# A hybrid attention trunk: contiguous rows per partition and another load order at the start, a finer warm-up, and a later due time for the layer border's transposes

## The chip, the cores and the metric

The kernel runs on one core of a Trainium2 chip. The metric is the device time of one execution in microseconds. The engines are TensorE (PE in the profile; its weight loads are PEld), VectorE (DVE), ScalarE (ACT), GpSimd (POOL) and SyncE (SP). DMAs are issued by an engine onto its own queue (SPq, ACTq) and carried out by 16 DMA engines.

## The reference, cut to what matters

Two layers over 256 tokens of 1024 channels; then a final RMSNorm:

```python
for layer in range(2):
    h = rms_norm(x, norm_g[layer])
    proj = einsum('btd,dc->btc', h, w_in[layer])          # w_in: 1024 x 3584
    sb_q, sb_k, sb_v, sb_g, mb_q, mb_k, mb_v, mb_g, mem_q, mem_g = split(proj)
    o_sb  = stick_breaking_attention(sb_q, sb_k, sb_v) * silu(sb_g)    # 6 heads of 64
    o_mb  = moba_attention(rotary(mb_q), rotary(mb_k), mb_v) * silu(mb_g)   # 6 heads
    mk, mv = split(einsum('bmd,dc->bmc', rms_norm(mem, mem_norm_g[layer]), w_mem_kv[layer]))
    o_mem = memory_attention(mem_q, mk, mv) * silu(mem_g)  # 4 heads, 256 memory tokens
    x = x + einsum('btc,cd->btd', concat([o_sb, o_mb, o_mem]), w_out[layer])
return rms_norm(x, final_norm_g)
```

All is in fp32. Besides the inputs the kernel is given x and mem transposed (xT, memT) and `gcols`, a 128 x 32 table of the four rows of gains: columns 0 to 7 are norm_g of layer 0, with row p, column k holding gain 128k + p; columns 16 to 31 are the memory gains.

## The kernel before, in words

**Split products.** A product of fp32 matrices is made of fp32r halves: each operand is split into a high part (a rounding cast) and a low part (the operand less its high part), and high x high, high x low and low x high are added up in PSUM. The activations are kept transposed, as `T` (a tile of 128 x 8 x 512: for each of 8 slices of 128 channels the high part in 256 columns and the low part in 256). In layer 0, `T` is x^T (tile `uT`, slices called xT0 to xT7) times the gain: `scale_hi` (L595, ScalarE, L248) makes the high part, `scale_lo` (L601, VectorE, L256) the low one. The rows' RMS factor is put in later, when a finished product leaves PSUM.

**Weights in chunks.** Every weight matrix comes in chunks of 128 partitions x 768 floats (384 KB; a few are 256 KB), in the order in which PE uses them. `dma_chunk` (L387) issues the next one on SyncE through `dma` (L332, so each issue shows as L333) into one of 5 buffers `raw`. `hi_task` (L405) casts it into the high half of one of 7 buffers `hl`, on ScalarE (L246) or VectorE (L267), as the planner finds; `lo_task` (L414) subtracts on VectorE (L252) and then calls `dma_chunk` again, since the `raw` buffer is free. The first piece, sb_qk, has 768 columns, so a chunk is one slice of 128 channels; its first two slices are cut in halves of 384 columns (chunks 0 to 3, 192 KB each), and chunk 4 is slice 2, chunk 5 slice 3, and so on.

**The layout of the channels.** `"(k p)"` in L355 and L428 lets partition p of slice k hold channel 128k + p, for w_in and x^T alike. A chunk's row in a partition is one run of memory (1.5 or 3 KB), and the next partition's run lies one row of w_in (14 KB) on. For x^T a run is one row of 1 KB.

**The start.** L436 to L446 issue the first loads in this order. On SyncE: gc (the table of gains, 16 KB), xT0, xT1, chunk 2, chunk 3, xT2, chunk 4, xT3, then xT4 and xT5 in one DMA. On ScalarE's queue: chunk 0, chunk 1. xT6 and xT7, the two halves of x and the constants follow when `dma_chunk` gets to chunks 7, 8 and 13 (L396 to L403). `main` (L980) clears `junk` on VectorE (L983) and runs 7 products of 128 x 512 in bf16 on it, whose result isn't used (the warm-up). Then come the products of sb_qk, slice by slice over six PSUM banks (L1053 to L1082): in slices 0 and 1 for three banks (one half chunk) at a time, with separate products of 256 columns; from slice 2 on with products of 512 and 256 columns.

**The order of the work.** A list planner written in the kernel (`Sched`, L82) decides in which order the instructions are issued on each engine, when the program is built: each task names what it needs, and the planner keeps a clock for each engine from estimated costs and landing times. A PE instruction of a side task is put `late` ns later than it could start by these estimates: `PE_LATE` = 100, and for the transposes at the layer border `NORM_LATE` (L32, L580). On the chip each engine runs its instructions strictly in that order and waits for semaphores.

**The layer border.** After layer 0's output projection, `norm_task` (L571) makes layer 1's `T` for two halves of tokens and two halves of channels: VectorE's normalised half-row `w` (L256, stt), four transposes on PE (L235), the high part on ScalarE and the low part on VectorE. In the meantime PE works on mk and mv of layer 1, which need only the memory tokens.

Of the kernel before, what the change touches and what calls it, by code (L numbers as in the profile page):

```python
# [7 lines left out]
F32 = mybir.dt.float32  # L8
FR = mybir.dt.float32r
BF = mybir.dt.bfloat16  # L10
AF = mybir.ActivationFunctionType
OP = mybir.AluOpType
# [5 lines left out]
KT = 8  # L18
# [10 lines left out]
KORD = (0, 1, 2, 3, 4, 5, 6, 7)  # L29
LAT_SAME, LAT_CROSS = 130.0, 240.0  # L30
PE_LATE = 100.0
NORM_LATE = 1200.0  # L32
P_H0 = -8
P_RX = 1
P_M0 = 12
P_RM = 12
P_M1 = 4
# [162 lines left out]
def hybrid_trunk(ctx: ExitStack, tc: tile.TileContext, x, mem, norm_g, w_in, w_mem_kv, w_out,  # L200
                 final_norm_g, xT, memT, gcols, consts, out):
    nc = tc.nc
# [35 lines left out]
    def act(out, in_, func=AF.Copy, **kw):  # L238
        c = 0.833 * _free(in_) + (50.0 if is_psum(in_) else 93.0)
        for a in ("scale", "bias"):  # L240
            if a in kw and not isinstance(kw[a], float):
                c += 93.0
        if "accum_out" in kw:
            c += 93.0
        if func == AF.Copy and not kw:
            nc.scalar.copy(out, in_)  # L246
        else:
            nc.scalar.activation(out, in_, func, **kw)  # L248
        S.op("act", c)
# [5 lines left out]
    def stt(out, a, s, b, op0, op1):  # L255
        nc.vector.scalar_tensor_tensor(out, a, s, b, op0=op0, op1=op1)  # L256
        S.op("dve", 1.0417 * _free(out) + (69.0 if isinstance(s, float) else 130.0))
# [12 lines left out]
    def R(*eng, **kw):  # L270
        kw["eng"] = [e if isinstance(e, tuple) else (e, 0.0) for e in eng]
        return kw

    def sb(name, shape, dt=F32):
        return cpool.tile(shape, dt, name=name)
# [2 lines left out]
    xs = sb("xs", [128, 2, D])  # L278
    cst = sb("cst", [128, 512])
    gc = sb("gc", [128, 32])  # L280
    identb = sb("identb", [128, 128], BF)
    masks = sb("masks", [128, 2, 128], BF)
    negT = sb("negT", [128, 128], FR)
# [48 lines left out]
    def dma(dst, src, name=None, q=None, now=0.0):  # L332
        (q or nc.sync).dma_start(dst, src)  # L333
        if q is None:
            S.T["sp"] = max(S.T["sp"], now) + SP_ISSUE
        t = queue(_free(dst) * 4 * dst.shape[0], dst.shape[-1] * 4, now)
        if name:
            S.ready[name] = t
# [13 lines left out]

    order = []
    for l in range(DEPTH):
        wi = w_in[l].rearrange("(k p) c -> p k c", p=128)  # L355
        wm = w_mem_kv[l].rearrange("(k p) c -> p k c", p=128)
        wo = w_out[l].rearrange("(k p) c -> p k c", p=128)
        names = ORDER[l] + ["wo0", "wo1", "wo2"]
        for n in names:
            if n in COLS:  # L360
                c, w = COLS[n]
                order.append(Piece(n, l, wi[:, :, c:c + w], w))
            elif n[:2] == "wo":
                c = 384 * int(n[2])
                w = min(384, D - c)
                order.append(Piece(n, l, wo[:, :, c:c + w], w))
            else:
                c = 256 * (n == "mv")
                order.append(Piece(n, l, wm[:, :, c:c + 256], 256))
# [17 lines left out]
    def dma_chunk(now=0.0, q=None):  # L387
        j = prog["dma"]
        if j >= len(chunks):
            return  # L390
        p, kk, c, w = chunks[j]
        n = len(kk)
        dma(raws[j % RAW][:, :n * w].rearrange("p (k c) -> p k c", c=w),
            p.src[:, kk[0]:kk[0] + n, c:c + w], ("raw", j), q, now)
        prog["dma"] += 1
        if j == X67_AT:  # L396
            load_xT(6, 8, now=now)
        for t, at in enumerate((X0_AT, X1_AT)):
            if j == at:
                dma(xs[:, t, :], x_r[:, t, :], ("x", t), now=now)  # L400
        if j == CST_AT:
            dma(cst, consts[:, 0:512], "cst", now=now)
            dma(S.res["w"].items[0][2][:, :256], consts[:, 512:768], "msk", now=now)  # L403

# [20 lines left out]

    x_r = x.rearrange("b (t p) d -> p (b t) d", p=128)
    mem_r = mem.rearrange("b (t p) d -> p (b t) d", p=128)
    xT_r = xT.rearrange("(k p) t -> p k t", p=128)  # L428
    memT_r = memT.rearrange("(k p) t -> p k t", p=128)
    out_r = out.rearrange("b (t p) d -> p (b t) d", p=128)  # L430
    def load_xT(k0, k1, q=None, now=0.0):
        dma(uT[:, k0:k1, :], xT_r[:, k0:k1, :], ("xT", k0), q, now)
        for k in range(k0 + 1, k1):
            S.ready["xT", k] = S.ready["xT", k0]

    dma(gc, gcols, "gc")  # L436
    dma_chunk(q=nc.scalar)
    load_xT(0, 1)
    dma_chunk(q=nc.scalar)
    load_xT(1, 2)  # L440
    dma_chunk()
    dma_chunk()
    load_xT(2, 3)
# [148 lines left out]
            S.mark(done + (q,))  # L592
        S.mark(done)

    def scale_hi(src, need, col, H, done):  # L595
        for k in range(KT):
            yield R("act", need=[need + (k,), "gc"])
            act(H[0][:, k, :], src[:, k, :], AF.Copy, scale=gc[:, col + k:col + k + 1])
            S.mark(done + ("hi", k))

    def scale_lo(src, need, col, H, done):  # L601
        for k in range(KT):
            yield R("dve", need=[done + ("hi", k)] + [("hi", 0)] * (k == 0))
            stt(H[1][:, k, :], src[:, k, :], gc[:, col + k:col + k + 1], H[0][:, k, :].bitcast(F32),
                OP.mult, OP.subtract)
            S.mark(done + (k,))

    def scale_task(src, need, col, H, done, prio):
        S.spawn(scale_hi(src, need, col, H, done), prio, S.cur.t)
        S.spawn(scale_lo(src, need, col, H, done), prio, S.cur.t)  # L610

    def load_memT(l):
        for q in range(4):
# [366 lines left out]
    def main():  # L980
        hT, mT = Ts
        yield R("dve")
        nc.vector.memset(junk, 0.0)  # L983
        S.op("dve", 150.0)
        _, (acc,) = yield R("pe", alloc=["bank"])
        for _ in range(7):
            mm(acc, junk[:, :128], junk, True, True)
        S.free("bank", acc)
        scale_task(uT, ("xT",), 0, hT, ("h", 0), P_H0)
        for t in range(2):  # L990
            S.spawn(row_stats(2, t, xs[:, t, :], "x", rcx, rbx), P_RX)
        S.spawn(rows_done("x", "rx"), P_RX)
# [1 line left out]
        def mem_loads():  # L994
            load_memT(0)
            dma(gb, mem_r[:, 0, :], ("mem", 0), now=S.cur.t)
            scale_task(uT, ("memT", 0), 16, mT, ("mT", 0), P_M0)
            S.spawn(rows_task(3, lambda t: gb, "mem", "rm", rcm, rbm), P_RM)

        late, given = [], set()  # L1000
# [6 lines left out]
        for l in range(DEPTH):  # L1007
# [75 lines left out]
            for i, p in enumerate(ORDER[l]):  # L1083
                if l == 0 and i == MEM_AT:
                    mem_loads()
                if l == 0 and set(ORDER[0][i:]) <= {"mk", "mv"} and not late:
                    late.append(scale_task(uT, ("memT", 1), 24, hT, ("mT", 1), P_M1))
                if p == "sb_q" and l == 1:
                    yield from T_piece(p, hT, 3, hneed, lambda c, acc: evac_T(l, "sb_q", c, acc, 0.125, rb, "rx"))
                elif p == "mk":  # L1090
                    yield from T_piece("mk", mT, 2, mneed, lambda c, acc: evac_T(l, "mk", c, acc, 1.0, rbm, "rm"))
                elif p == "mv":
                    yield from N_piece("mv", mT, mneed,
                                       lambda t, acc: evac_v(l, "mv", t, acc, rcm[:, t:t + 1], 4, "rm"))
                elif p == "sb_k":
                    yield from T_piece(p, hT, 3, hneed, lambda c, acc: evac_T(l, "sb_k", c, acc, 1.0, rb, "rx"))
                elif p in ("sb_v", "mb_v"):
                    yield from N_piece(p, hT, hneed, lambda t, acc: evac_v(l, p, t, acc, rr_(t), 6, "rx"))
                elif p == "mem_q":
                    yield from T_piece(p, hT, 2, hneed,  # L1100
                                       lambda c, acc: evac_T(l, "mem_q", c, acc, 0.125, rb, "rx"))
                elif p == "mb_q":
                    yield from N_piece(p, hT, hneed, lambda t, acc: rope_task(
                        l, "mb_q", t, acc, rr_(t, True) if l == 0 else 0.125))
                elif p == "mb_k":
                    S.spawn(rope_turn(l), 2, S.cur.t)
                    yield from N_piece(p, hT, hneed, lambda t, acc: rope_task(
                        l, "mb_k", t, acc, rr_(t) if l == 0 else 1.0))
                if {"mk", "mv"} <= set(ORDER[l][:i + 1]) and not S.res["F%d" % l].items and l not in given:
                    given.add(l)  # L1110
                    for f in range(4):
                        S.free("F%d" % l, mT[2][:, 2 * f:2 * f + 2, :].rearrange("p k c -> p (k c)").bitcast(F32))
                if p in GATES:
                    yield from T_piece(p, hT, sum(map(len, GATES[p])), hneed, lambda c, acc: gate_evac(
                        l, p[:-2], c, acc, [g for g in GATES[p] if c in g][0]))

            if l == 0 and not late:
                late.append(scale_task(uT, ("memT", 1), 24, hT, ("mT", 1), P_M1))

            def xneed(k):  # L1120
                return [("mx", l, k)]
# [71 lines left out]
```

## Time and profile before

| | |
|---|---|
| time, median of 3 runs | 279.24 us (278.77 to 279.37) |
| profiled execution | 279.69 us |
| its span, first to last instruction | 277.9 us |
| mean granted TensorE clock | 0.997 |
| PE busy | 97 % of the span |
| VectorE busy | 83 % |
| ScalarE busy | 66 % |
| DMA, mean rate | 218 GB/s |

The profile is of one execution, whose time outside the span is 1.8 us. In its rows a group reads: start, duration, engine, line, operation, output <- inputs, shape and count; the bracket behind has the engine's idle time before it and what ended that. L230 is the helper of all products, L333 that of all DMAs, L246, L248, L252, L256 and L267 those of casts, scalings and subtractions, so groups are told apart by their tiles.

### The profile page before, as it was taken

Reading aid. Unit: us, or ns where it says so; the run is one execution under the profiler, and the core shown is the slowest. Engines: PE = TensorE matmul, PEld = TensorE weight load, DVE = VectorE, ACT = ScalarE, POOL = GpSimd, SP = SyncE. Lnnn points to the kernel's source line nnn. Section 1 sums busy time; section 2 is a strip of 40 time slices with the busy share of each in tenths; the row PEclk is TensorE's granted clock in tenths of the full one; section 3 lists DMA queues with packets and bytes.
Section 4 is the critical chain, followed back from the end, with each engine's and each line's share of the span. In section 5 each row is a group of like instructions: output and inputs, shape, how many; then the busy total and the mean of one; then the engine's idle time right before and its main releaser. Section 6 shows DMA issues by size and latency. Waiting matters only on the chain.

```text
span 277.9 us, 4990 instructions
## 1 busy us (share of the span) xinstructions
PE 270.2 (97%) x1713; PEld 242.5 (87%) x1713; DVE 230.6 (83%) x517; ACT 184.2 (66%) x413; POOL 3.6 (1%) x10
## 2 busy tenths in 40 slices
PE   7999999999999999999999999999999999999991
PEld 4889999987978897998988989988888899889991
DVE  3868999998998999995879757979889989686173
ACT  3778999967565876772776437569559977443053
POOL 0020000100000000000000000000000000000000
PEclk9999999999999999999999999999999999999998
DMA  7999969686878887784465884853598895770004
GB/s 209 345 397 374 355 187 291 186 275 210 261 237 258 254 217 226 245 221 145 148 235 191 275 255 141 261 165 108 143 297 276 263 282 167 213 241 2 0 0 152
DMA packets 45866, 60.50 MB, mean 218 GB/s; under 512 B 3345, under 2 KB 42641, under 8 KB 45841
## 3 DMA queue, kind: packets, MB, share of 16 engines
q1 hardware_dynamic: 44976, 58.36, 67.2%
q0 software_dynamic: 288, 1.05, 1.3%
q10 hardware_dynamic: 576, 0.79, 0.8%
q8 instruction: 13, 0.21, 0.4%
q14 instruction: 13, 0.10, 0.1%
HBM read 53.89 MB, written 6.29 MB: 217 GB/s over the span
## 4 chain that ended last, share of the span: by engine, by line
PE 92%; DMA 3%; DVE 2%; ACT 1%; issue 0%; SPq 0%; DVEq 0%; ACTq 0%
PE bank L230 91%; DMA raw<-in_w_in_dram 2%; DMA uT<-xT_dram 1%; PE bank L235 1%; DVE hl L252 1%; DVE xs L252 0%; ACT ss L248 0%; ACT junk L248 0%; ACT hl L246 0%; DVE w L256 0%; ACT T L248 0%; SPq L333 0%; DVE ss L527 0%; DVE xs L260 0%; DVEq L1189 0%
## 5 line engine op out<-in xcount | busy, mean ns | idle before, releaser
L252 DVE TENSOR_TENSOR hl<-raw,hl 128x768 fp32r<-128x768 f32 (+2 forms) x112 | 101.4, 912 | 11.5 <-ACT hl L246 10.9
L230 PE MATMUL bank<-T,hl 128*128 128x512 f32 (+1 forms) x582 | 107.3, 341 | 0.4 <-ACT T L248 0.4
L230 PEld LDWEIGHTS bank<-T,hl 128*128 128x128 f32 x582 | 89.5, 190 | 14.5 <-issue 1.6
L246 ACT CAST hl<-raw 128x768 fp32r<-128x768 f32 (+2 forms) x101 | 80.5, 811 | 23.2 <-PE bank L230 7.6
L230 PE MATMUL bank<-hl,T 128*128 128x384 f32 (+1 forms) x448 | 82.3, 338 | 0.0
L230 PEld LDWEIGHTS bank<-hl,T 128*128 128x128 f32 x448 | 76.5, 188 | 1.9 <-issue 0.2
L230 PE MATMUL bank<-hl,mxhi 128*128 128x384 f32 (+1 forms) x192 | 44.9, 318 | 0.0
L230 PEld LDWEIGHTS bank<-hl,mxhi 128*128 128x128 f32 x192 | 33.3, 189 | 0.8 <-issue 0.4
L230 PE MATMUL bank<-hl,mxlo 128*128 128x384 f32 (+1 forms) x96 | 30.4, 317 | 0.0
L248 ACT ACTIVATE junk<-xs 128x384 bf16<-128x384 f32 (+2 forms) x16 | 8.4, 526 | 19.2 <-DVE xs L252 18.5
L248 ACT ACTIVATE w<-bank,st 128x256 f32<-128x256 f32 (+1 forms) x40 | 17.3, 448 | 2.7 <-DVE st L719 2.7
L230 PEld LDWEIGHTS bank<-hl,mxlo 128*128 128x128 f32 x96 | 18.1, 189 | 0.0
L248 ACT ACTIVATE ga<-ga 128x768 f32<-128x768 f32 (+1 forms) x24 | 15.2, 635 | 1.7 <-DVE ga L256 1.3
L246 ACT COPY gT<-bank 128x256 f32<-128x256 f32 x16 | 6.0, 374 | 13.1 <-PE bank L230 13.1
L248 ACT ACTIVATE T<-uT,gc 128x256 fp32r<-128x256 f32 x24 | 11.5, 510 | 4.4 <-DMA uT<-xT_dram 4.4
L252 DVE TENSOR_TENSOR xs<-bank,xs 128x384 f32<-128x384 f32 (+1 forms) x12 | 6.1, 511 | 9.7 <-PE bank L230 9.7
L719 DVE TENSOR_REDUCE st<-bank 128x1 f32<-128x256 f32 (+1 forms) x40 | 13.3, 370 | 0.0
L749 DVE STREAM_TRANSPOSE D<-w 128x384 f32<-128x384 f32 (+1 forms) x20 | 12.5, 623 | 0.0
L256 DVE SCALAR_TENSOR_TENSOR T<-uT,gc,T 128x256 fp32r<-128x256 f32 x24 | 11.3, 486 | 0.6 <-ACT T L248 0.5
L248 ACT ACTIVATE a<-a 128x384 f32<-128x384 f32 x24 | 11.6, 527 | 0.0
L260 DVE TENSOR_SCALAR w<-w,st 128x256 f32<-128x256 f32 (+1 forms) x40 | 11.1, 325 | 0.0
L252 DVE TENSOR_TENSOR gT<-bank,gT 128x256 f32<-128x256 f32 x16 | 6.7, 420 | 4.8 <-ACT gT L246 4.7
(112 smaller groups left out, 251.6 us busy)
## 6 DMA issues: line engine op xcount, KB each, us to landing
raw<-in_w_in_dram SPq DMA_DIRECT2D x70, 384.0 KB, 4.8
raw<-in_w_out_dram SPq DMA_DIRECT2D x20, 384.0 KB, 4.3
raw<-in_w_mem_kv_dram SPq DMA_DIRECT2D x8, 384.0 KB, 3.6
Z<-D SPq DMA_DIRECT2D x8, 384.0 KB, 4.5
T<-Z SPq DMA_DIRECT2D x24, 96.0 KB, 4.5
uT<-memT_dram SPq DMA_DIRECT2D x8, 256.0 KB, 4.7
Z<-D SPq DMA_DIRECT2D x4, 512.0 KB, 3.4
T<-Z SPq DMA_DIRECT2D x16, 128.0 KB, 5.1
```

Source lines behind the costliest of these rows:

```text
L230: nc.tensor.matmul(out, lhsT=lhsT, rhs=rhs, start=start, stop=stop, **kw)
L235: nc.tensor.transpose(out, in_, idt)
L246: nc.scalar.copy(out, in_)
L248: nc.scalar.activation(out, in_, func, **kw)
L252: nc.vector.tensor_tensor(out, a, b, op=op)
L256: nc.vector.scalar_tensor_tensor(out, a, s, b, op0=op0, op1=op1)
L260: nc.vector.tensor_scalar(out, a, s, None, op0=op)
L719: nc.vector.tensor_reduce(st[:, t:t + 1], sc[:, r0:r1], axis=AX.X, op=OP.max, negate=True)
L749: nc.vector.transpose(o, w[:, :n * 128].rearrange("p (m j r) -> p m j r", j=4, r=32))
```

## The change

1. In layer 0, w_in and x^T are viewed as `"(p k)"`: partition p holds channels 8p to 8p + 7, and slice k is channel 8p + k. The sum over channels is the same, taken in another order. A chunk's run in a partition is as long as before (from slice 2 on 3 KB), but the next partition's lies eight rows on (112 KB for w_in, 8 KB for x^T). xT4 and xT5 in one DMA are now runs of 2 KB. Layer 1, w_mem_kv, w_out and mem^T stay at `"(k p)"`.
2. The gains of layer 0 come from norm_g itself in the same layout, 8 floats for a partition (32 bytes), into a new tile gx. gc is still wanted for the memory gains; its load moves to just ahead of the constants.
3. The first loads. SyncE: xT0, xT1, chunk 2, chunk 3, xT2, chunk 4, xT3, xT4 and xT5. ScalarE's queue: gx, chunk 0, chunk 1.
4. The warm-up is 30 products of 128 x 128 in place of 7 of 128 x 512, and only 128 columns of `junk` are cleared.
5. `NORM_LATE` goes from 1200 to 1800 ns.

```diff
-NORM_LATE = 1200.0
+NORM_LATE = 1800.0
...
+    gx = sb("gx", [128, KT])
...
-        wi = w_in[l].rearrange("(k p) c -> p k c", p=128)
+        wi = w_in[l].rearrange("(k p) c -> p k c" if l else "(p k) c -> p k c", p=128)
...
         if j == CST_AT:
+            dma(gc, gcols, "gc", now=now)
             dma(cst, consts[:, 0:512], "cst", now=now)
...
-    xT_r = xT.rearrange("(k p) t -> p k t", p=128)
+    xT_r = xT.rearrange("(p k) t -> p k t", p=128)
...
-    dma(gc, gcols, "gc")
-    dma_chunk(q=nc.scalar)
     load_xT(0, 1)
+    dma(gx, norm_g[0].rearrange("(p k) -> p k", p=128), "gx", nc.scalar)
     dma_chunk(q=nc.scalar)
     load_xT(1, 2)
+    dma_chunk(q=nc.scalar)
     dma_chunk()
     dma_chunk()
     load_xT(2, 3)
...
-    def scale_hi(src, need, col, H, done):
+    def scale_hi(src, need, g, gneed, H, done):
         for k in range(KT):
-            yield R("act", need=[need + (k,), "gc"])
-            act(H[0][:, k, :], src[:, k, :], AF.Copy, scale=gc[:, col + k:col + k + 1])
+            yield R("act", need=[need + (k,), gneed])
+            act(H[0][:, k, :], src[:, k, :], AF.Copy, scale=g[:, k:k + 1])
...
-        nc.vector.memset(junk, 0.0)
-        S.op("dve", 150.0)
+        nc.vector.memset(junk[:, :128], 0.0)
+        S.op("dve", 100.0)
         _, (acc,) = yield R("pe", alloc=["bank"])
-        for _ in range(7):
-            mm(acc, junk[:, :128], junk, True, True)
+        for _ in range(30):
+            mm(acc[:, :128], junk[:, :128], junk[:, :128], True, True)
         S.free("bank", acc)
-        scale_task(uT, ("xT",), 0, hT, ("h", 0), P_H0)
+        scale_task(uT, ("xT",), gx, "gx", hT, ("h", 0), P_H0)
...
-            scale_task(uT, ("memT", 0), 16, mT, ("mT", 0), P_M0)
+            scale_task(uT, ("memT", 0), gc[:, 16:24], "gc", mT, ("mT", 0), P_M0)
```

Because the planner works with estimated times, the edits also move instructions. On VectorE the cast of chunk 2 now stands ahead of the subtraction for chunk 1, and the low part of T's slice 0 ahead of that for chunk 0; the cast of chunk 3 goes from VectorE to ScalarE; the first evacuations of sb_q come before the split of chunk 13. At the layer border the second group of transposes stands behind 12 more products of mk (before: 8), the third behind 10 of mv (before: 4), the fourth behind 8 of mv's second half (before: 0), and one cast of a weight chunk goes from ScalarE to VectorE. The semaphore on which the load of xT4 and xT5 waits is now that of chunk 2's landing; before, it was that of xT1's.

More of the change, by code (lines that the diff above doesn't have):

```diff
@@ L593, in norm_task, with scale_lo, scale_task @@
         S.mark(done)
-    def scale_hi(src, need, col, H, done):
+    def scale_hi(src, need, g, gneed, H, done):
         for k in range(KT):
-            yield R("act", need=[need + (k,), "gc"])
-            act(H[0][:, k, :], src[:, k, :], AF.Copy, scale=gc[:, col + k:col + k + 1])
+            yield R("act", need=[need + (k,), gneed])
+            act(H[0][:, k, :], src[:, k, :], AF.Copy, scale=g[:, k:k + 1])
             S.mark(done + ("hi", k))
-    def scale_lo(src, need, col, H, done):
+    def scale_lo(src, need, g, gneed, H, done):
         for k in range(KT):
             yield R("dve", need=[done + ("hi", k)] + [("hi", 0)] * (k == 0))
-            stt(H[1][:, k, :], src[:, k, :], gc[:, col + k:col + k + 1], H[0][:, k, :].bitcast(F32),
-                OP.mult, OP.subtract)
+            stt(H[1][:, k, :], src[:, k, :], g[:, k:k + 1], H[0][:, k, :].bitcast(F32), OP.mult, OP.subtract)
             S.mark(done + (k,))
-    def scale_task(src, need, col, H, done, prio):
-        S.spawn(scale_hi(src, need, col, H, done), prio, S.cur.t)
-        S.spawn(scale_lo(src, need, col, H, done), prio, S.cur.t)
+    def scale_task(src, need, g, gneed, H, done, prio):
+        S.spawn(scale_hi(src, need, g, gneed, H, done), prio, S.cur.t)
+        S.spawn(scale_lo(src, need, g, gneed, H, done), prio, S.cur.t)
     def load_memT(l):
@@ L1086, in main @@
                 if l == 0 and set(ORDER[0][i:]) <= {"mk", "mv"} and not late:
-                    late.append(scale_task(uT, ("memT", 1), 24, hT, ("mT", 1), P_M1))
+                    late.append(scale_task(uT, ("memT", 1), gc[:, 24:32], "gc", hT, ("mT", 1), P_M1))
                 if p == "sb_q" and l == 1:
@@ L1117, in main @@
             if l == 0 and not late:
-                late.append(scale_task(uT, ("memT", 1), 24, hT, ("mT", 1), P_M1))
+                late.append(scale_task(uT, ("memT", 1), gc[:, 24:32], "gc", hT, ("mT", 1), P_M1))
             def xneed(k):
```

## The prediction

> **What bounds the kernel now.** I read the page first (busy time, shares of the chain), then the chain in order of time, then the timeline of the first 16 us, and last the layer border, the one later place where PE waits.
>
> ```profile
> span 277.9 us, 4990 instructions
> ...
> PE 270.2 (97%) x1713; PEld 242.5 (87%) x1713; DVE 230.6 (83%) x517; ACT 184.2 (66%) x413; POOL 3.6 (1%) x10
> ...
> PE 92%; DMA 3%; DVE 2%; ACT 1%; issue 0%; SPq 0%; DVEq 0%; ACTq 0%
> ```
>
> TensorE (PE) is the bound: 270.2 of 277.9 us. The change removes no product of the computation, so it can only gain where PE stands still or runs slowly. The profiled execution took 279.69 us, 1.8 more than its span and 0.45 above the median of the three runs (279.24). The chain in order of time opens so:
>
> ```profile
> 0.74 0.39 SPq L333
> ...
> 1.18 2.94 DMA uT<-xT_dram
> ...
> 4.21 0.52 ACT T L248
> ...
> 4.78 44.34 PE bank L230 x275
> ```
>
> The first x^T rows sit on SyncE's queue behind gc, land at 1.18 + 2.94 = 4.12, ScalarE scales them, and the first product runs at 4.78. Beside it, from the timeline:
>
> ```profile
> 0.86 0.27 DVE L983 MEMSET junk<- 128x256 uint32 x1 [0.86 <-PEq L1177]
> ...
> 1.19 3.17 PE L230 MATMUL bank<-junk 128*128 128x512 bf16 x7 [1.19 <-DVE junk L983]
> ...
> 3.30 0.36 DVE L267 CAST hl<-raw 128x384 fp32r<-128x384 f32 x1 [2.17 <-DMA raw<-in_w_in_dram]
> ...
> 4.78 11.45 PE L230 MATMUL bank<-T,hl 128*128 128x256 f32 x65 [0.42 <-ACT T L248]
> ...
> 5.16 0.56 DVE L252 TENSOR_TENSOR hl<-raw,hl 128x384 fp32r<-128x384 f32 x1
> ...
> 6.87 0.84 DVE L267 CAST hl<-raw 128x384 fp32r<-128x384 f32 x2 [0.76 <-DMA raw<-in_w_in_dram]
> ...
> 10.95 1.74 ACT L246 CAST hl<-raw 128x768 fp32r<-128x768 f32 x2
> ```
>
> The warm-up ends at 4.36 and PE idles 0.42 us before the first product. Chunk 0 (`raw0`) has landed by 3.30, before x^T; chunk 2 only at 6.87; chunk 5 begins its ScalarE copy at 10.95. Two stretches of equal length, with PE's instruction count in brackets, and a single matmul:
>
> ```profile
> core 0: us, PE busy (x), PEclk, DMA share, GB/s
> 5.15:6.20 1.05, 1.05 (x6) 1.00 1.00 273
> 6.60:7.65 1.05, 1.05 (x11) 1.00 0.97 320
> ```
> ```profile
> 11.92 0.43 PE L230 MATMUL bank<-T,hl 128*128 128x512 f32 x1
> ```
>
> Both stretches hold products of 256 columns: 6 touch the first, 11 the second. So PE runs at about half speed until some moment between 6.2 and 6.6 (0.21 us a product, from the warm-up's 0.42 us per 512 columns, against 0.12 later). The matmul at 11.92 is the first that needs chunk 5, whose copy ends at 10.95 + 0.84 = 11.79: a slack of 0.13 us. PE never stalls here, but the DMA stream is right behind it.
>
> The layer border (timeline, with the chain's DMA row first):
>
> ```profile
> 135.44 5.45 DMA raw<-in_w_in_dram
> ```
> ```profile
> 140.97 0.84 ACT L246 CAST hl<-raw 128x768 fp32r<-128x768 f32 x1 [0.32 <-DMA raw<-in_w_in_dram]
> ...
> 142.82 0.75 DVE L256 SCALAR_TENSOR_TENSOR w<-xs,ss,gb 128x512 f32<-128x512 f32 x1 [1.44 <-ACT ss L248]
> ...
> 143.62 0.66 PE L235 MATMUL bank<-cst,w 128*128 128x128 f32 x4 [0.33 <-DVE w L256]
> ```
>
> A late w_in chunk holds ScalarE, which then is late with the row statistics; VectorE's normalised half-row is ready at 143.57, and PE, in order, stands 0.33 us in front of the second group of four transposes (0.5 with the drain of the product before).
>
> **The change part by part.**
>
> *First loads.* x^T's first rows take gc's place as SyncE's first DMA, issued at 0.74 instead of 1.18. gx (4 KB in 32-byte pieces) becomes ScalarE's first DMA, so chunk 0 is issued one issue later, at about 1.2. Prices from these rows (the last number is the median us from issue to landing):
>
> ```profile
> raw<-in_w_in_dram ACTq DMA_DIRECT2D x2, 192.0 KB, 2.8
> raw<-in_w_in_dram SPq DMA_DIRECT2D x2, 192.0 KB, 4.7
> ...
> gc<-gcols_dram SPq DMA_DIRECT2D x1, 16.0 KB, 2.0
> ```
>
> gx is not in this trace; nearest is gc, equally 128 small pieces: 2.0 us, so about 2.8. Its bounds are 0 and 2.9 us (x^T's first row), landing by 3.7 at worst, still not last. x^T lands near 3, its scaling ends near 3.6. Chunk 0 is now last: nearest is the DMA that stood behind gc, 2.94 us, so 1.2 + 2.9 = 4.1 (bounds 3.7 with ScalarE's 2.5 to 3.1 around the median of 2.8, and 4.7 if it meets SyncE's queue as chunk 2 did). Add the cast of 0.36: first product at about 4.5 instead of 4.78, **0.3 us earlier** (0.7 to -0.3). While PE runs at half speed, an earlier start gains only half its length.
>
> *The stream behind it.* The bytes up to chunk 5 are the same, less 12 KB. The stream starts better:
>
> ```profile
> 0.00:2.00 2.00, 0.81 (x2) 0.28 (x3) 0.27 (x1) 1.26 (x1) 0.41 (x5) 1.00 0.06 9
> 2.00:4.00 2.00, 2.00 (x6) 0.60 (x4) 0.67 (x2) 0.02 (x1) 0.00 (x0) 1.00 0.98 310
> 4.00:6.00 2.00, 1.58 (x6) 1.23 (x6) 1.50 (x4) 1.32 (x3) 0.00 (x0) 1.00 1.06 259
> ```
>
> Before 2 us only 9 GB/s flow, gc's small pieces leading. With 128 KB of x^T leading instead, I put the stream 0.2 to 0.4 us ahead. Against that, the changed program's instruction order lets x^T rows 4 and 5 wait for chunk 2's landing (a semaphore reused; before, for the second x^T load), and chunk 5 is queued behind them on SyncE. Chunks 3 and 4 and two x^T loads (832 KB, over 2 us at these rates) are then still in flight, and they cover it; if the cover goes, chunk 5 is some 0.5 late. Because of the slack of 0.13, what PE keeps is the smaller of its earlier start and the stream's lead: **-0.2 us** (bounds +0.4 and -0.5).
>
> *VectorE's order.* The low part of chunk 1 (5.16 now) moves behind the cast of chunk 2, which waits for a landing. Behind that cast stand the low parts of chunks 1 and 2. If chunk 2 landed at 6.84 again, the low part would end at 6.87 + 0.36 + 0.56 = 7.8; PE wants it at 7.2 to 7.4. Chunk 2 now starts in third place, not fourth, so I take 5 to 6.3 and no wait.
>
> *Warm-up.* The memset is a quarter as long; PE starts about 0.15 us sooner. Price of a 128-column step:
>
> ```profile
> 36.42 0.84 PE L230 MATMUL bank<-identb,masks 128*128 128x128 bf16 x12
> ```
>
> Twelve take 0.84 us with a drain of 0.22, so 0.056 each at full speed, 0.107 at half speed (0.42 / 4). Thirty end between 2.7 and 4.3, ahead of the first product at 4.5: it hides behind the wait for chunk 0. If chunk 0 came at 3.7, the warm-up's end would be the later, by 0.1 to 0.2. The Trainium skill (TensorE: Matmul & The Clock Gate, Part 1) says that the clock rises after one busy window of about 3.4 us that runs freely. By that, closing a gap of 0.42 gains nothing of itself and the moment differs from run to run; the trace agrees so far that it rose 5 to 5.4 us after the first matmul, which is more than one window.
>
> *gc's later place and the evacuations of sb_q before chunk 13's split.* One SyncE issue (0.39) ahead of the constants and chunk 8; PE meets these chunks over 1 us after they are ready, which hides it. Taken at 0; 0.4 if the cover is gone.
>
> *NORM_LATE.* In the changed order of PE the second group of transposes comes four products later (0.70 us: two of 512, two of 256 columns), the third and fourth likewise later. PE then reaches the second group at 143.13 + 0.70 = 143.8, after 143.57: **-0.49 us** in this execution. The next two are fed by
>
> ```profile
> 145.29 0.74 DVE L256 SCALAR_TENSOR_TENSOR w<-xs,ss,gb 128x512 f32<-128x512 f32 x1
> ...
> 147.75 0.74 DVE L256 SCALAR_TENSOR_TENSOR w<-xs,ss,gb 128x512 f32<-128x512 f32 x1
> ```
>
> Replaying VectorE's new order with these durations (one more cast goes to VectorE), they end at 146.4 and 149.3, and PE arrives at 146.7 and 149.6: 0.3 us to spare each. But the wait hangs on one slow landing, 5.45 us where w_in's median is 4.8; 0.65 sooner and there is no wait to remove. For the median run I take **-0.2** (bounds 0 and -0.5).
>
> *Sum.* In the profiled execution 279.69 - 0.2 - 0.49 = 279.0. Against the median: 279.24 - 0.2 - 0.2 = **278.8 us**.
>
> **The rivals.**
>
> *All of it, and the clock early.* If the clock rises before the first product, about 7 products save 0.1 each; with the stream's full lead the start gives 0.5 and the border 0.4: 278.3. For it: the half speed is in the trace, and the profiled run was a slow one. Against: the 0.13 slack. Chance 0.25.
>
> *It moves nothing.* The stream, not the start, sets chunk 5; chunk 2 is late and the low part of chunk 1 waits behind it; the border shows no wait in most runs: 279.2 (279.0 to 279.5). Chance 0.2.
>
> *The wider pitch reads slower: slower than before.* w_in's rows under one DMA go from 14 KB apart to 112 KB, x^T's from 1 to 8. Landing times of 384 KB:
>
> ```profile
> raw<-in_w_in_dram SPq DMA_DIRECT2D x70, 384.0 KB, 4.8
> raw<-in_w_out_dram SPq DMA_DIRECT2D x20, 384.0 KB, 4.3
> raw<-in_w_mem_kv_dram SPq DMA_DIRECT2D x8, 384.0 KB, 3.6
> ```
>
> The pitches are 14, 4 and 2 KB. If pitch were the reason, it is 1.2 us in 2.8 doublings, and three more doublings add 1.3 us. At chunk 5 that leaves PE waiting 1.3 - 0.13 - 0.3 = 0.9: 279.24 + 0.9 - 0.2 = 279.9 (up to 280.4). It decides from about 0.45 us of added landing on (no gain at the start), and at 1.2 it is slower by 0.2%. Against: queue depth explains these rows as well. The Trainium skill (DMA: Bandwidth & Descriptors, Latency and other measured facts) has copies at 512 KiB pitch at 207 GB/s of 214 and a real loss only from 2 MiB; by that the 112 KB cost at most 0.2 us here. No run shows it yet. Chance 0.2.
>
> **How the numbers follow.** Forecast (278.5 to 279.1) 0.35, all 0.25, nothing 0.2, slower 0.2. 0.2% is 0.56 us, about what a measurement here tells from no change: faster means below 278.68, slower above 279.80. Faster: 0.25 + a third of 0.35 = 0.37. Slower: most of the pitch rival, 0.17. Same: 0.46. The range 278.1 to 280.0 takes in all cases but the ends of the first and the last.
>
> **What would show it.** First product near 4.5 with chunk 0's cast, not x^T, as its releaser; x^T's first landing near 3; PE at chunk 5 no later than 11.8; no PE wait at the second group of transposes. Wrong if chunk 0 lands after 4.4, if VectorE's cast of chunk 2 is followed by a PE gap, or if w_in's landings exceed 5.5 us in layer 0.

## The result and the profile after

The changed kernel takes **281.38 us** (median of 5 runs, 280.48 to 281.65) against 279.24 (278.77 to 279.37): ratio 1.0068, 95% interval 1.0045 to 1.0091. It is slower, and 1.4 us above the top of the forecast range. The profiled execution took 281.65 us, with a span of 279.9.

The page of the changed kernel, the lines that answer to those of before:

```profile
span 279.9 us, 5036 instructions
...
PE 270.8 (97%) x1736; PEld 245.5 (88%) x1736; DVE 230.8 (82%) x517; ACT 184.4 (66%) x413; POOL 3.2 (1%) x10
...
PE 96%; DMA 2%; ACT 1%; DVE 0%; DVEq 0%; issue 0%
```

Averages tell nothing here: PE has 0.6 us more of busy time and its share is the same. The chain in order of time does (start, length, what):

```profile
1.19 4.59 DMA raw<-in_w_in_dram
...
5.81 0.37 DVE hl L267
...
6.32 45.19 PE bank L230 x275
```

Chunk 0's landing is now what the first product waits for, as the forecast said, but it takes 4.59 us and not 2.9: the first product runs at 6.32, not at 4.5, and 1.54 later than before. How the bytes came in is seen in stretches of 1 us; the last column is GB/s, and PEclk, the granted clock, stands two columns ahead of it. First before, then after:

```profile
2.00:3.00 1.00, 1.00 (x4) 0.43 (x3) 0.00 (x0) 0.02 (x1) 0.00 (x0) 1.00 0.87 265
3.00:4.00 1.00, 1.00 (x4) 0.17 (x2) 0.67 (x2) 0.00 (x0) 0.00 (x0) 1.00 1.08 355
4.00:5.00 1.00, 0.58 (x2) 0.23 (x2) 0.50 (x2) 0.79 (x2) 0.00 (x0) 1.00 1.05 234
...
8.00:9.00 1.00, 1.00 (x8) 0.86 (x7) 0.93 (x3) 0.54 (x2) 0.00 (x0) 1.00 0.99 357
9.00:10.00 1.00, 1.00 (x7) 0.91 (x6) 0.67 (x2) 0.95 (x3) 0.00 (x0) 1.00 1.02 392
10.00:11.00 1.00, 1.00 (x6) 0.78 (x6) 1.00 (x3) 0.93 (x3) 0.00 (x0) 1.00 0.98 381
```
```profile
2.00:3.00 1.00, 1.00 (x13) 1.00 (x11) 0.00 (x0) 0.01 (x1) 0.00 (x0) 1.00 0.66 149
3.00:4.00 1.00, 1.00 (x13) 0.97 (x11) 0.00 (x0) 0.51 (x1) 0.00 (x0) 1.00 0.74 145
4.00:5.00 1.00, 0.14 (x3) 0.00 (x0) 0.00 (x0) 0.00 (x0) 0.00 (x0) 1.00 0.88 276
7.00:8.00 1.00, 1.00 (x7) 0.97 (x6) 1.00 (x4) 0.97 (x3) 0.00 (x0) 0.59 0.84 309
8.00:9.00 1.00, 1.00 (x7) 1.00 (x6) 1.00 (x4) 0.57 (x2) 0.00 (x0) 0.50 0.99 163
9.00:10.00 1.00, 1.00 (x6) 1.00 (x6) 0.87 (x3) 1.00 (x2) 0.00 (x0) 0.50 0.88 230
10.00:11.00 1.00, 1.00 (x5) 0.76 (x5) 0.98 (x2) 0.01 (x1) 0.00 (x0) 0.70 0.94 217
```

Two things are to be seen. The loads are slow in two stretches: 294 KB in the 2 us from 2 on instead of 620, and 610 KB in the 3 us from 8 on instead of 1130. In both, x^T is in flight: its first slices in the one, the DMA of slices 4 and 5 in the other (which before was issued 1.9 us earlier, so these three us don't hold quite the same loads). And the granted clock falls to one half from 7 to 10.6, after PE has stood idle for 2.17 us. How far PE is behind by then, and when it gets chunk 5, is read from the timeline: the first product of 384 columns (the next piece, mb_k, is under way), before and after, and ScalarE's copy of chunk 5:

```profile
22.54 1.75 PE L230 MATMUL bank<-hl,T 128*128 128x384 f32 x9
```
```profile
24.93 1.40 PE L230 MATMUL bank<-hl,T 128*128 128x384 f32 x7
```
```profile
12.82 0.83 ACT L246 CAST hl<-raw 128x768 fp32r<-128x768 f32 x1 [0.25 <-DMA raw<-in_w_in_dram]
```

PE is 2.39 us behind at that mark; chunk 5's copy starts 1.87 later than before (12.82 against 10.95). Chunk 5 was late in its issue already. SyncE's queue, before and after (the last row of each begins with chunk 5):

```profile
4.14 0.91 SPq L333 DMA_DIRECT2D uT<-xT_dram  x2
5.17 3.36 SPq L333 DMA_DIRECT2D raw<-in_w_in_dram  x3
```
```profile
3.25 0.33 SPq L334 DMA_DIRECT2D raw<-in_w_in_dram  x1
5.39 1.51 SPq L334 DMA_DIRECT2D uT<-xT_dram  x2
7.06 1.94 SPq L334 DMA_DIRECT2D raw<-in_w_in_dram  x3
```

SyncE issues chunk 5 at 7.06 and not at 5.17, 1.89 later. It stands 1.8 us for x^T's landing before it issues xT3 (whose semaphore is now that of xT1; before, it was that of xT0), and 0.8 us for a chunk of w_in before xT4 and xT5. So what lands late here holds up PE's first product and also the issue of later loads.

At the end the spans differ by 2.0; the 0.4 between is the layer border, where the wait for VectorE's `w` is gone. All that PE waits for in the changed kernel (us in total, times, longest):

```profile
PE bank L230 <- DVE hl L267: 2.2, 1, 2.2
PE bank L230 <- DVE junk L984: 1.0, 1, 1.0
```

So the loss is made in the first 11 us. Open were its cause (the layout, or the order of the loads), which of the two arrays, and what turns slow loads into time: the late start, the halved clock, or the stream itself.

### The profile page after: what moved, and what is told of

It reads as the page before. It is cut to its first block, busy times and chain, and to the rows that moved or that the text cites. A ratio compares the mean times of both kernels' runs of the same rounds, so it can differ in the third digit from the quotient of the medians.

```text
span 279.9 us, 5036 instructions
## 1 busy us (share of the span) xinstructions
PE 270.8 (97%) x1736; PEld 245.5 (88%) x1736; DVE 230.8 (82%) x517; ACT 184.4 (66%) x413; POOL 3.2 (1%) x10
## 3 DMA queue, kind: packets, MB, share of 16 engines
q0 software_dynamic: 288, 1.05, 1.2%
## 4 chain that ended last, share of the span: by engine, by line
PE 96%; DMA 2%; ACT 1%; DVE 0%; DVEq 0%; issue 0%
PE bank L230 95%; DMA raw<-in_w_in_dram 2%; PE bank L235 1%; ACT junk L248 0%; ACT ss L248 0%; DVE xs L252 0%; ACT L207 0%; DVE hl L267 0%; DVE xs L260 0%; DVEq L1190 0%
## 5 line engine op out<-in xcount | busy, mean ns | idle before, releaser
L267 DVE CAST hl<-raw 128x768 fp32r<-128x768 f32 (+1 forms) x11 | 5.6, 513 | 5.2 <-DMA raw<-in_w_in_dram 4.9
L248 ACT ACTIVATION_READ_ACCUMULATOR w<-bank,st 128x1 f32 x40 | 8.4, 210 | 0.0
```

The costliest lines, as they stand in the source:

```text
L267: nc.vector.tensor_copy(out, in_)
```

## The experiments

Each was measured in 5 rounds beside the kernel before on the same chip; ratios are to that kernel, and are not the quotients of the two medians. In e3, e4, e8, e10, e11, e13 and e16 the two layouts don't match, so the products leave out the right pairing of channels; the amount of work is the same.

| kernel | median us | before, same chip | ratio (95% interval) |
|---|---|---|---|
| the changed kernel | 281.38 | 279.24 | 1.0068 (1.0045 to 1.0091) |
| e1 old layout | 279.94 | 279.41 | 1.0019 (0.9998 to 1.0039) |
| e2 layout only | 280.77 | 279.41 | 1.0052 (1.0035 to 1.0069) |
| e3 old x^T layout | 280.22 | 279.41 | 1.0017 (0.9997 to 1.0038) |
| e4 old w_in layout | 281.71 | 279.41 | 1.0078 (1.0057 to 1.0099) |
| e13 x^T rows 2 KB apart | 280.56 | 279.19 | 1.0043 (1.0025 to 1.0062) |
| e8 x^T rows 4 KB apart | 280.79 | 279.46 | 1.0040 (1.0021 to 1.0060) |
| e10 first slices wide | 281.65 | 279.19 | 1.0070 (1.0044 to 1.0096) |
| e11 last slices wide | 280.64 | 279.19 | 1.0049 (1.0031 to 1.0067) |
| e5 changed, longer warm-up | 281.48 | 279.46 | 1.0057 (1.0032 to 1.0082) |
| e16 e10, longer warm-up | 281.21 | 279.24 | 1.0083 (1.0061 to 1.0106) |
| e12 e1, longer warm-up | 280.10 | 279.19 | 1.0020 (1.0006 to 1.0034) |
| e6 due time only | 280.02 | 279.46 | 0.9999 (0.9973 to 1.0024) |
| e14 order only | 280.74 | 279.24 | 1.0054 (1.0030 to 1.0078) |
| e9 another order | 280.60 | 279.46 | 1.0036 (1.0018 to 1.0053) |
| e15 before, longer warm-up | 279.36 | 279.24 | 1.0006 (0.9994 to 1.0018) |

**Layout or order (e1, e2).** e1 is the changed kernel with the old views:

```diff
-        wi = w_in[l].rearrange("(k p) c -> p k c" if l else "(p k) c -> p k c", p=128)
+        wi = w_in[l].rearrange("(k p) c -> p k c", p=128)
-    xT_r = xT.rearrange("(p k) t -> p k t", p=128)
+    xT_r = xT.rearrange("(k p) t -> p k t", p=128)
-    dma(gx, norm_g[0].rearrange("(p k) -> p k", p=128), "gx", nc.scalar)
+    dma(gx, gcols[:, 0:8], "gx", nc.scalar)
```

> The changed kernel with x^T and layer 0's w_in back at the old layout, the gains taken as columns 0 to 7 of the table (still 32 bytes a partition, still first on ScalarE's queue). Every engine's order is that of the changed kernel. Theory A (the wide rows read slowly at the start, and the clock falls because PE then idles): chunk 0 lands near 4.1, first product near 4.5, no second half-speed stretch, 278.5 to 279.1 us. Theory B (the order of the loads is to blame: gx ahead of chunk 0, x^T and chunk 2 beside it): chunk 0 lands after 5.4 as in the changed kernel, 281 to 281.6 us.

e2 is the reverse, the kernel before with the new views:

```diff
-    dma(gc, gcols, "gc")
+    dma(gx, norm_g[0].rearrange("(p k) -> p k", p=128), "gx")
```

> The kernel before with only the new layout: gx stands in gc's place at the head of SyncE's queue, gc goes to the constants; load order, warm-up of 7 x 512 columns and the border's due time are the old ones. Theory A: chunk 0 lands after 5 us instead of 3.3, the first product comes about 1.5 us later and the clock falls again, 280.7 to 281.8 us. Theory B: 279.0 to 279.5 us.

The layout alone costs 0.52%, and all the rest of the change with the old layout 0.19% (an interval that reaches zero). Together they make about the 0.68% of the change. In e1 chunk 0 takes 2.93 us and the first product runs at 4.64; in e2 it runs at 5.69. Theory A holds in its main point, theory B doesn't. But e1's time lies above what A gave, and e2 goes another way than A said: there x^T's first rows, 3.87 us in flight, are the last to come, not chunk 0, and the granted clock doesn't fall.

**Which array (e3, e4).** One of the two lines of e1 alone is undone: x^T's view in e3, w_in's in e4.

> The changed kernel with x^T alone back at the old layout (the products of layer 0 then pair the channels of x^T with the wrong rows of w_in; nothing is left out, and the amount of work is the same). Theory A1 (the x^T rows 8 KB apart are the slow ones): 278.5 to 279.3 us. Theory A2 (the w_in rows 112 KB apart are the slow ones): 281 to 281.6 us. Both share it: 279.5 to 280.7.

> The changed kernel with layer 0's w_in alone back at the old layout (channels paired wrongly again, the same amount of work). Theory A1 (x^T): 281 to 281.6 us. Theory A2 (w_in): 278.5 to 279.3 us. Theory B: as the changed kernel, 281 to 281.6.

The third and fourth us of e3, then of e4:

```profile
2.00:3.00 1.00, 1.00 (x13) 1.00 (x11) 0.00 (x0) 0.01 (x1) 0.00 (x0) 1.00 0.89 220
3.00:4.00 1.00, 1.00 (x12) 1.00 (x11) 0.00 (x0) 0.51 (x1) 0.00 (x0) 1.00 1.05 371
```
```profile
2.00:3.00 1.00, 1.00 (x13) 1.00 (x11) 0.00 (x0) 0.01 (x1) 0.00 (x0) 1.00 0.64 148
3.00:4.00 1.00, 1.00 (x12) 1.00 (x11) 0.00 (x0) 0.47 (x1) 0.00 (x0) 1.00 0.65 87
```

With w_in's rows 112 KB apart and x^T contiguous the loads run at up to 371 GB/s, and the time is that of e1 (1.0017 and 1.0019). With x^T's rows 8 KB apart and the old w_in they run at 148 and 87, and the time is that of the changed kernel. (By its median alone, 280.22, e3 would fall into "both share it"; but e1, where nothing is wide, took 279.94, and the two ratios agree.) The wider pitch of the two is harmless; **x^T's 1 KB rows, 8 KB apart, are the slow loads.**

**How far apart (e13, e8).** x^T alone is viewed in quarters or halves, all else is the changed kernel:

```diff
-    xT_r = xT.rearrange("(p k) t -> p k t", p=128)
+    xT_r = xT.rearrange("(a p b) t -> p a b t", a=4, b=2)
```

(a=2, b=4 in e8; the DMA indexes a and b.)

> The changed kernel with the rows of x^T 2 KB apart in one DMA (four quarters of channels, partition p holds 2p and 2p + 1 of each; channels are paired wrongly, the amount of work is the same). If the slowness grows with the distance: between 1 KB (first loads 220 and 371 GB/s in the third and fourth us) and 4 KB (188 and 218): 279.9 to 280.7 us. If contiguous rows alone are fast: 280.6 to 281.5.

> The changed kernel with the rows of x^T 4 KB apart in one DMA instead of 8 KB (two halves of channels, partition p holds 4p to 4p + 3 of each; the products of layer 0 pair the channels wrongly, the amount of work is the same). If the slowness grows with the distance of the rows: between the old layout of x^T (first loads at 220 to 370 GB/s, 279.3 to 280.2 us) and 8 KB (90 to 150 GB/s, 281.4): 280.0 to 280.9. If only 8 KB apart is slow: as the old layout, 279.3 to 280.2. If any break of the contiguous 128 KB is slow: 281.0 to 281.8.

e13, then e8:

```profile
2.00:3.00 1.00, 1.00 (x13) 1.00 (x11) 0.00 (x0) 0.01 (x1) 0.00 (x0) 1.00 0.75 225
3.00:4.00 1.00, 1.00 (x12) 1.00 (x11) 0.00 (x0) 0.51 (x1) 0.00 (x0) 1.00 1.03 280
```
```profile
2.00:3.00 1.00, 1.00 (x13) 1.00 (x11) 0.00 (x0) 0.01 (x1) 0.00 (x0) 1.00 0.70 188
3.00:4.00 1.00, 1.00 (x12) 1.00 (x11) 0.00 (x0) 0.51 (x1) 0.00 (x0) 1.00 0.85 218
```

The fourth us falls in order: 371, 280, 218, 145 GB/s at 1, 2, 4 and 8 KB (e3, e13, e8, the changed kernel). These are single executions, e13's the fastest of its twelve runs; the ends of the row are borne out by others with the same issue order (326, 340 and 320 GB/s in e1, e11 and e12, whose first slices are contiguous; 87, 158, 134 and 144 in e4, e5, e10 and e16 at 8 KB). The third us shows the order less well (220, 225, 188, 149). The loads slow down with the distance. The times (1.0017, 1.0043, 1.0040, 1.0068) go the same way, but only those of 1 and 8 KB are told apart by their intervals. Why it is so isn't shown by these runs. The DMA engines' busy share falls too (0.74 in the changed kernel's fourth us, 1.05 in e3's), so in part they stood idle.

**Which of the two stretches (e10, e11).** x^T's slices 0 to 3 have the new view and 4 to 7 the old one in e10; in e11 the reverse:

```diff
-        dma(uT[:, k0:k1, :], xT_r[:, k0:k1, :], ("xT", k0), q, now)
+        dma(uT[:, k0:k1, :], (xT_r if k0 < 4 else xT_o)[:, k0:k1, :], ("xT", k0), q, now)
```

> The changed kernel with x^T's slices 0 to 3 at the new layout (rows 8 KB apart) and slices 4 to 7 at the old one (some channels are read twice and others not at all; the amount of work is the same). Theory D (each time that wide x^T rows are in flight the stream of loads loses about 1 us, and PE can't run ahead of the stream): chunk 0 lands near 5.8 as in the changed kernel, chunk 5 near 11.5 instead of 12.8, time 280.2 to 280.9 us. Rival (the late first product is all of the loss): 281.2 to 281.7 us.

> The mirror of the last: slices 0 to 3 of x^T at the old layout, 4 to 7 at the new one. Theory D: first product near 4.6 to 5, the stream slows only from about 8 to 10 us, chunk 5 lands near 11.5 to 12, time 280.2 to 280.9 us. Rival (the late first product is all of the loss): 279.3 to 280.0 us, as the old layout.

e11 fits theory D, e10 doesn't: the first stretch alone makes the whole loss. SyncE's wait comes with it: in e10 too it issues chunk 5 only at 7.17 (e11: 6.01, e1: 5.69). The two don't add up (0.51% and 0.30% over e1, together 0.49%). A likely reason, argued and not shown, is that PE which is already late isn't delayed again by a chunk that comes late while it lags. The rival falls by e11, where the first product runs at 4.86 and 0.49% is lost all the same, though its interval overlaps e1's a little; PE there waits 0.56 us for chunk 5's copy.

**Late start, halved clock or stream (e5, e16, e12).** The only edit is the length of the warm-up, in the changed kernel (e5), in e10 (e16) and in e1 (e12):

```diff
-        for _ in range(30):
+        for _ in range(52):
```

> The changed kernel with 52 products of 128 columns in the warm-up instead of 30, enough at half speed (52 x 0.107 = 5.6 us from 0.99 on) to reach the first product, which the loads hold until 6.3 as before. Theory C (the half speed after the start is the price of TensorE's idle 2.2 us): the half-speed stretch of the changed kernel from 7.1 to 10.6 is gone, every product after 8 us runs at full speed, 280.2 to 280.8 us. Rival (the clock comes up at its own moment whatever the warm-up does): 281.0 to 281.7 us, half speed until about 10.

e5, two stretches and all that PE waits for:

```profile
7.00:8.00 1.00, 1.00 (x10) 0.97 (x9) 1.00 (x4) 0.99 (x3) 0.00 (x0) 1.00 0.82 297
8.00:9.00 1.00, 1.00 (x9) 0.95 (x8) 1.00 (x4) 0.58 (x2) 0.00 (x0) 1.00 0.84 193
```
```profile
PE bank L230 <- DVE junk L984: 1.0, 1, 1.0
PE bank L230 <- ACT hl L246: 0.3, 1, 0.3
PE bank L230 <- DVE hl L267: 0.2, 1, 0.2
```
```profile
24.51 1.73 PE L230 MATMUL bank<-hl,T 128*128 128x384 f32 x9
```

Theory C was right about the clock and wrong about its price. The halved clock is gone (1.00 where the changed kernel has 0.59 and 0.50), but the median is the same as without the edit (1.0057 against 1.0068, the intervals overlap almost wholly). PE now runs into the stream: it waits for ScalarE's copy of a chunk, and at the mark it is only 0.42 ahead of the changed kernel, where half of the 3.5 slow us would be 1.7. The halved clock lay largely beside loads that were late anyway. The changed kernel's own runs agree: 3.4 us at half speed take 0.006 from the mean granted clock, so the two runs with 0.998 and 0.997 were without that stretch, and they still took 280.48 and 281.12.

> The kernel with x^T's slices 0 to 3 at the new layout and 4 to 7 at the old one, now with 52 products in the warm-up (channels mismatched as there, the amount of work is the same). If its loss is the late start and the half speed that follows TensorE's idle time: 280.3 to 281.0 us, products at full speed from 8 us on. If its loads set the pace: 281.2 to 281.8 us with waits of TensorE for chunks in the trace.

Here the one profiled execution shows a gain, at the mark first in e10, then in e16:

```profile
24.94 1.23 PE L230 MATMUL bank<-hl,T 128*128 128x384 f32 x6
```
```profile
23.93 1.73 PE L230 MATMUL bank<-hl,T 128*128 128x384 f32 x9
```

That is 1.0 us, and the profiled times are 281.61 and 280.67. The runs don't bear it out: 280.67 to 282.61, six of them, with a median of 281.21, at the lower end of the second expectation, though without the waits for chunks that it named. What the clock is worth in e10 stays open.

> The changed kernel with the old layout, and a warm-up of 52 products, so that PE starts late (about 6.2 to 6.6) though the loads are fast. It starts 1.7 later than the old layout does but runs no half-speed stretch of 2 us after it, which gives about 0.9 back. Theory D: 280.4 to 281.0 us, and the first product of 384 columns, which stands at 22.6 us with the old layout and at 24.9 in the changed kernel, at 23.1 to 23.8. Rival (the late first product is all of the loss): 281.2 to 281.8 us.

Below both expectations: PE started at 5.18, not at 6.3, since the clock came up during the warm-up and shortened it (22 of its products touch the fifth us, against 12 in e5); so the run tells nothing of a start at 6.3. It took 0.2% more than the kernel before, as e1 does.

**The due time (e6).**

```diff
-NORM_LATE = 1200.0
+NORM_LATE = 1800.0
```

> The kernel before with the border's due time alone at 1800. If the removed wait is real in most executions: 278.7 to 279.1 us, and no wait of TensorE for VectorE's w in the trace. If it was peculiar to the profiled execution of the kernel before: 279.2 to 279.5 us. Not more than 279.6.

No change that can be told: 0.9999, with an interval of a quarter per cent to either side. The median of 280.02 lies above both expected ranges (12 runs, 278.99 to 281.56). The profiled execution shows one source of such spread. Up to the border e6's PE runs the products of the kernel before in the same order, from 4.86 on (before: 4.78). But its products of 256 columns come every 0.21 us until 8.65, where before they come every 0.12 us from 6.4 on, at a PEclk of 1.00 in both. At the mark it is 1.03 us later (23.57). e3 runs at half speed until 9.4 (e1 until 6.7), and its mark is 23.96 against 22.58. So a single profile's mark can hold a us or more that is set by the moment at which PE comes to full speed, and the argument on the layout rests on the ratios. e2 keeps the due time of 1200 and doesn't wait either; its second half-row and the transposes that use it:

```profile
143.54 0.75 DVE L256 SCALAR_TENSOR_TENSOR w<-xs,ss,gb 128x512 f32<-128x512 f32 x1 [1.42 <-ACT ss L248]
```
```profile
144.45 0.60 PE L235 MATMUL bank<-cst,w 128*128 128x128 f32 x4
```

The half-row ends at 144.29 and PE comes at 144.45. Of four profiled kernels with 1200 (before, e2, e14, e15) only the first shows the wait.

**The order of the loads (e14, e9).** e14 is the kernel before with the new start, gx taken from the table, and gc ahead of the constants:

```diff
-    dma(gc, gcols, "gc")
-    dma_chunk(q=nc.scalar)
     load_xT(0, 1)
+    dma(gx, gcols[:, 0:8], "gx", nc.scalar)
     dma_chunk(q=nc.scalar)
     load_xT(1, 2)
+    dma_chunk(q=nc.scalar)
```

> The kernel before with the new order of the first loads alone (x^T first on SyncE, gx, as 32 bytes a partition out of the table, first on ScalarE, gc ahead of the constants); layout, warm-up and due time are the old ones. If the 0.5 us that stay with the old layout come from the order and what the planner makes of it: 279.6 to 280.2 us. If they come from the warm-up's small steps: 279.0 to 279.5.

Slower than expected, and in the profiled execution not by its start: the first product runs at 4.77, as before, and PE is at the mark at 22.34, 0.2 ahead of before. Far behind it, in layer 1, the timeline of e14 has

```profile
225.53 0.83 ACT L246 CAST hl<-raw 128x768 fp32r<-128x768 f32 x1 [2.33 <-DMA raw<-in_w_in_dram]
...
228.89 0.96 DVE L256 SCALAR_TENSOR_TENSOR ga<-gT,ga 128x768 f32<-128x768 f32 x1 [2.39 <-ACT ga L248]
...
234.50 0.55 DVE L267 COPY sb_v<-bank 128x384 f32<-128x384 f32 x1
...
235.10 1.09 PE L230 MATMUL bank<-wT,sb_v 128*64 128x128 f32 x12 [0.51 <-DVE sb_v L267]
```

PE stands 0.5 us for the copy of sb_v. The engines' order is that of the kernel before here; what differs is a landing. ScalarE waits 2.33 us for a chunk of w_in (before: 1.45), VectorE 2.39 for ScalarE (before: 1.19), and the copy comes at 234.50 instead of 233.94, while PE, without the border's wait, is 0.6 ahead of before. Whether the edit has to do with that landing isn't shown. No other profiled kernel here shows this wait. It is a third of the 1.5 us by which the medians differ, and the runs reach from 279.18 to 282.74. So e14 isn't the price of the order alone, and its split from e1 stays open.

e9 (the old layout, chunk 0 again first on ScalarE's queue, gx second on SyncE's) was meant as a better start:

```diff
     load_xT(0, 1)
-    dma(gx, gcols[:, 0:8], "gx", nc.scalar)
     dma_chunk(q=nc.scalar)
+    dma(gx, gcols[:, 0:8], "gx")
     load_xT(1, 2)
```

> The changed kernel with the old layout, and chunk 0 again first on ScalarE's queue, gx second on SyncE's behind x^T's first rows. Both x^T's first rows and chunk 0 then lead a queue: chunk 0 lands near 3.3, gx near 3.6, scaling to 4.1, first product near 4.2 with the warm-up's end at 4.16, so no idle gap: 278.4 to 279.0 us. If the start is not worth what it moves: 279.2 to 279.9, as the old layout alone.

It missed. The first product came at 4.72, and PE then waited for the low parts of chunks:

```profile
PE bank L230 <- DVE hl L252: 1.1, 2, 0.6
```

Chunk 2 landed at about 6.7, hardly earlier than in the kernel before, and behind its cast on VectorE stood the low part of chunk 1: the wait that the forecast named for the changed kernel, where it didn't come.

**The kernel before with a warm-up without a gap (e15).** 36 products of 128 columns in place of 7 of 512, nothing else.

> The kernel before with a warm-up of 36 products of 128 columns and nothing else, which at half speed reaches from 0.99 to 4.84, where its first product starts. If TensorE's idle 0.42 us sets how late the clock comes up in some executions, the upper half of the runs goes: 278.7 to 279.1 us in the median. If not: 279.1 to 279.5. If the loads are what bounds the start anyway, the same.

No change that can be told (1.0006). Of all the versions none beats the kernel before.

## Why the prediction was wrong

- **What bounds the kernel** was right: nothing but PE's waits and slow stretches moved the time, and chunk 0 did take x^T's place as the last before the first product.
- **First loads: the term that failed.** The forecast let chunk 0 land 2.9 us after its issue, at 4.1 (bounds 3.7 and 4.7); it took 4.59 us, and landed at 5.78. The price came from rows in which x^T's rows were contiguous, and holds for them: in e1, the same program with the old layout, chunk 0 takes 2.93 us and lands at 4.11. With x^T's rows 8 KB apart the third and fourth us moved 294 KB instead of 620.
- **The stream behind it** was put 0.2 to 0.4 us ahead and came 1.87 behind at chunk 5. The forecast had seen that chunk 5 stands on SyncE's queue behind a load that waits for a landing, and counted on the loads in flight to cover it, or else on some 0.5 us. The cover failed: SyncE stood for x^T, and chunk 5 was issued 1.89 late. That xT3 waits for xT1 now was missed. With the old layout the same order issues it 0.52 late (e1, 5.69), as the forecast's fallback had it. The slack of 0.13 us, which the forecast took from the trace, is used up: PE waits for chunks' copies in e5 and e11.
- **The rival of the wider pitch** had the right kind of mechanism and sign, and a price of 1.3 us at chunk 5, where 1.87 was measured; its time (up to 280.4) was still too short. But it rested on the wrong array. It read w_in's landings against their pitch; e3 shows that w_in's 112 KB cost nothing, and x^T's step from 1 to 8 KB was named and not priced. The Trainium skill (DMA: Bandwidth & Descriptors, Latency and other measured facts) gives 207 GB/s at a row pitch of 512 KiB, where 214 is the full rate, and a larger loss from 2 MiB on, for tiles of 16 KiB a partition. e3 agrees for w_in, with no loss at 112 KB; x^T's 1 KB rows, slow at 8 KB in e4, are a case that the table doesn't hold.
- **VectorE's order:** no wait in the changed kernel, as forecast, but by luck. Chunk 2 landed at about 6.5 and was cast at 7.35, where 5 to 6.3 was expected; PE, which began 1.54 late, came to the low parts later as well. e9 has the wait.
- **Warm-up:** its end was hidden, as forecast. That the idle time behind it would bring the clock down again was not foreseen; e5 shows that little hung on it.
- **NORM_LATE:** the wait is gone in the profiled execution, as forecast for it (the two spans close by 0.4 from the mark to the end). That the new value did it isn't shown: e2, e14 and e15 don't wait with the old one. The 0.2 us taken for the median is less than e6 can tell. A wait in one profile isn't yet a wait in the median.
- **The chances:** the cases with a gain held 0.6, on the reading that issue order sets landing times. What was missing was a doubt about the shape of each DMA that the change re-lays, the small one too.

## What to carry to other kernels

When a change re-lays an array, price the DMAs of each array by its own piece and distance, not by the nearest big one: here 1 MB of x^T in 1 KB rows, 8 KB apart, cost more than 14 MB of w_in in rows 112 KB apart. Look also at what stands behind such a load in its queue: here the next loads waited for it to land, and chunk 5 was issued 1.89 us late. Where the stream of loads has 0.1 us of slack, as at this kernel's start, a slow stretch of 2 us shows in the time, and a longer warm-up didn't buy it back (e5). And look through all waits of PE before a part alone is taken for that part's price: e14's extra wait stands 230 us behind its edit.

## What the runs showed of the hardware

- Loads of 128 rows of 1 KB, with chunks beside them: the fourth us moved 371, 280, 218 and 145 GB/s with rows 1, 2, 4 and 8 KB apart (one execution each), while w_in's rows of 1.5 and 3 KB at 112 KB were no slower than at 14 KB (e3 and e1: 1.0017 and 1.0019).
- An idle gap of 2.17 us, after 3.2 us of warm-up, brought the granted clock to 0.50 not in the gap but 0.8 us after PE had begun again; it lasted from 7.1 to 10.6 (changed kernel). With the gap at 0.2 us (e5) it stayed at 1.00.
- PEclk also reads 1.00 before PE has come to full speed: e4, after a gap of 2.04 us, shows no fall, but its products of 256 columns come every 0.21 us from the first one at 6.41 to about 10, and then every 0.12.
- gx, 4 KB in pieces of 32 bytes, took 2.6 us to land, against gc's 2.0 for 16 KB; its bounds held.
